# RG-LRU gates in a decoder layer: both gates of a block as the columns of one matmul, high and low half of its input in one stack of 128 rows

## The chip, the core and the metric

One NeuronCore of one Trainium2 chip runs the whole kernel. The metric is the device time of one execution in microseconds. The kernel before was timed in three runs: median 2068.51 us, from 2068.23 to 2069.02. A profile of one more execution goes with them; every row of a trace below is from it.

## The reference

One layer of a decoder: 512 tokens of 2048 features, float32. One input projection makes `rg_x`, `rg_gate`, `q`, `k` and `v`. The changed part is the recurrent group, 1024 features wide, whose two gates are matrices of 16 blocks of 64x64:

```python
def _rglru_group(rg_x, rg_gate, conv_w, conv_b, wa, ba, wx, bx, lam):
    u = _causal_dwconv(rg_x, conv_w, conv_b)
    ub = u.reshape(B, S, RG_BLOCKS, RG_BLOCK_DIM)          # 16 blocks of 64
    r = sigmoid(einsum('bsgi,gij->bsgj', ub, wa).reshape(B, S, RG_WIDTH) + ba)
    ig = sigmoid(einsum('bsgi,gij->bsgj', ub, wx).reshape(B, S, RG_WIDTH) + bx)
    log_a = RG_C * r * log_sigmoid(lam)
    a = exp(log_a)
    mult = sqrt(-expm1(2.0 * log_a))
    h = scan(h = a * h + mult * ig * u)                    # along the tokens
    return h * gelu(rg_gate)
```

Beside it a differential attention of 8 heads with two softmaxes each; then an output projection over both groups, a layer norm, a gated MLP of width 5632 with a causal convolution of width 3, and a second layer norm.

## The kernel before

Activations lie transposed: a tile is 128 features by 512 tokens. Float32 accuracy is had from a cheaper matmul type by splitting each operand into a high half (a copy in the rounded type) and a low half (the difference): `split`, ScalarE for the copy (L108), VectorE for the difference (L109). A product is then three matmuls, high by high, high by low, low by high (`mm3`, L115). Weights come by DMA as 128x1024 raw tiles, are split by the same two lines into `whi` and `wlo`, and are used four matmul triples per 512 columns.

A list `PLAN` sets the order of the first stage: projections of `v`, `q` and `k` of a head, `rg_x` ("x"), `rg_gate` ("g") and, four times, "rec": the recurrence over two tiles of 128 features. Attention and recurrence are generators that are started some microseconds of modelled time later, so that their instructions fall among the matmuls of the next projections. A scheduler then orders each engine's instructions by modelled times; each engine takes them in that order.

- `rg_in` (the "x" step) makes `u` of one tile: ScalarE from PSUM (L448), three convolution steps on VectorE (L452), then a split into a 128x512 `hi` and `lo`.
- `recurrence` takes two tiles, four gates. For each gate of each tile there is a 128x128 matrix with two 64x64 blocks on its diagonal and zeros elsewhere, split into high and low: three matmuls and one sigmoid of 128x512 from PSUM (L468).
- After the four sigmoids: exp (L474) and tanh (L476) on ScalarE, `ig * u` on GpSimd (L480), two steps on VectorE (L482, L483), a square root on ScalarE (L486), a product (L488) and the scan (L490, tile `hh`) on VectorE.
- Sigmoid, exp with tanh, and square root need different function tables; ScalarE loads a table (1.28 us) at each change.

The blocks of the four gate matrices of one recurrence are one DMA of 128x512, `gate_w`, split once.

```python
for i, (uu, s) in enumerate(us):
    for g in range(2):
        c = slice((2 * i + g) * P, (2 * i + g + 1) * P)
        pg = bank()
        mm3(pg, (hi[:, c], lo[:, c]), s, True, True)
        gt = t_tile(F32, "gt")
        nc.scalar.activation(gt, pg, AF.Sigmoid, bias=col((C_BA, C_BX)[g] + j0 + i))
        gates.append(gt)
```

Of the kernel before, what the change touches and what calls it, by code (L numbers as in the profile page):

```python
# [10 lines left out]
F32 = mybir.dt.float32  # L11
F32R = mybir.dt.float32r
AF = mybir.ActivationFunctionType
ALU = mybir.AluOpType
PSUM = bass.MemoryType.PSUM

P = 128
# [4 lines left out]
RGT = RG // P  # L22
H = 8
DH = 64
# [12 lines left out]
C_BA = C_CONVB + RGT  # L37
C_BX = C_BA + RGT
# [5 lines left out]
C_FB = C_FW + 2 * FT * 3  # L44
C_LQ = C_FB + 2 * FT
NC_ = C_LQ + 4 * DH


A_BUFS = 56
# [22 lines left out]
def f32(ap):  # L72
    return ap.bitcast(F32)
# [3 lines left out]
def trunk_kernel(ctx, tc, xT, w_qkg, w_v, gate_w, w_out0, w_out, w_up0, w_up, w_down, ln2, consts, out):  # L77
    nc = tc.nc
# [10 lines left out]
    def bank():  # L89
        return psum.tile([P, S], F32, tag="ps", bufs=8, name="ps")  # L90

    def a_tile(dt=F32R, name="a"):
        return act.tile([P, S], dt, tag="a", bufs=A_BUFS, name=name)

    def t_tile(dt=F32, name="t"):
        return tmp.tile([P, S], dt, tag="t", bufs=T_BUFS, name=name)
# [7 lines left out]
    def split(src, hi=None, lo=None, mk=a_tile):  # L104

        hi = mk(F32R, "hi") if hi is None else hi
        lo = mk(F32R, "lo") if lo is None else lo
        nc.scalar.activation(hi, src, AF.Copy)  # L108
        nc.vector.tensor_tensor(lo, src, f32(hi), ALU.subtract)  # L109
        return hi, lo  # L110

    def mm3(ps, w, x, first, last, onto=False):

        for n, (a, b) in enumerate(((w[0], x[0]), (w[0], x[1]), (w[1], x[0]))):
            nc.tensor.matmul(  # L115
                ps, a, b, start=first and n == 0, stop=last and n == 2, skip_group_check=onto
            )
# [82 lines left out]

    cst = const.tile([P, NC_], F32, name="cst")

    def col(i, n=1):
        return cst[:, i : i + n]
# [126 lines left out]
    def proj():  # L331

        ps = bank()
        for half in range(2):
            parts = W.take()
            for kk in range(8):
                kt = half * 8 + kk
                hi, lo = parts[kk // 4]
                c = slice((kk % 4) * P, (kk % 4 + 1) * P)
                mm3(ps, (hi[:, c], lo[:, c]), x[kt], kt == 0, kt == KT - 1)  # L340
                if kt < KT - 1:
                    tick(TK)
        return ps
# [101 lines left out]
    def rg_in(j):  # L445
        ps = proj()
        uu = t_tile(F32, "uu")
        nc.scalar.activation(  # L448
            uu, ps, AF.Identity, scale=col(C_CONVW + 4 * j + 3), bias=col(C_CONVB + j)
        )  # L450
        for t in range(1, 4):
            nc.vector.scalar_tensor_tensor(  # L452
                uu[:, t:], ps[:, : S - t], col(C_CONVW + 4 * j + 3 - t), uu[:, t:],
                ALU.mult, ALU.add,
            )
        return uu, split(uu, mk=t_tile)

    def recurrence(j0, us, w):

        hi, lo = w  # L460
        gates = []
        for i, (uu, s) in enumerate(us):
            for g in range(2):
                c = slice((2 * i + g) * P, (2 * i + g + 1) * P)
                pg = bank()
                mm3(pg, (hi[:, c], lo[:, c]), s, True, True)
                gt = t_tile(F32, "gt")
                nc.scalar.activation(gt, pg, AF.Sigmoid, bias=col((C_BA, C_BX)[g] + j0 + i))  # L468
                gates.append(gt)
        ms, as_ = [], []  # L470
        for i in range(2):
            j, r = j0 + i, gates[2 * i]
            a = t_tile(F32, "a")
            nc.scalar.activation(a, r, AF.Exp, scale=c8[:, j : j + 1])  # L474

            nc.scalar.activation(r, r, AF.Tanh, scale=nc8[:, j : j + 1])  # L476
            as_.append(a)
        for i in range(2):
            uu, ig, r, a = us[i][0], gates[2 * i + 1], gates[2 * i], as_[i]
            nc.gpsimd.tensor_tensor(ig, ig, uu, ALU.mult)  # L480
            m = t_tile(F32, "m")
            nc.vector.tensor_tensor(m, a, a, ALU.mult)  # L482
            nc.vector.scalar_tensor_tensor(m, m, 1.0, r, ALU.add, ALU.mult)  # L483
            ms.append(m)
        for m in ms:
            nc.scalar.activation(m, m, AF.Sqrt)  # L486
        for i in range(2):
            nc.vector.tensor_tensor(ms[i], ms[i], gates[2 * i + 1], ALU.mult)  # L488
            hh = a_tile(F32, "hh")
            nc.vector.tensor_tensor_scan(hh, as_[i], ms[i], 0.0, ALU.mult, ALU.add)  # L490
            mix[j0 + i] = hh
        yield 0.0
# [57 lines left out]
    us = {}  # L550
# [87 lines left out]
    for dt in range(KT):  # L638
# [14 lines left out]
        if dt == 1:  # L653
            pair = [bank(), bank()]
            for u in range(KT // 4):
                parts = W.take()
                for kk in range(4):
                    i = 4 * u + kk
                    tick(2 * TK)
                    assert ms[i] is not None  # L660
                    hi, lo = parts[kk // 2]
                    for o in range(2):
                        c = slice((kk % 2 * 2 + o) * P, (kk % 2 * 2 + o + 1) * P)
# [11 lines left out]
        for n in range(2):  # L675
            parts = W.take()
            for kk in range(8):
                i = n * 8 + kk
                hi, lo = parts[kk // 4]
                c = slice((kk % 4) * P, (kk % 4 + 1) * P)  # L680
                mm3(ps, (hi[:, c], lo[:, c]), ms[i], i == 0, i == KT - 1)
        residual(dt, ps)
    for tok in halves:
        for dt in range(KT - 2, KT):
            ps = bank()
            for i in range(KT):
                hi, lo = wl[dt - KT + 2][i // 8][i % 8 // 4]
                c = slice((i % 4) * P, (i % 4 + 1) * P)
# [230 lines left out]
    for i in range(2, PLAIN):  # L919
        pss = []  # L920
        for g in range(2):
            ps = bank()
            for half in range(2):
# [4 lines left out]
                for kk in range(8):  # L928
                    kt = half * 8 + kk
                    hi, lo = parts[kk // 4]  # L930
                    c = slice((kk % 4) * P, (kk % 4 + 1) * P)
# [47 lines left out]
    at = 0  # L979
# [70 lines left out]
def _layout(inputs):  # L1050
    import numpy as np

    g = {k: np.asarray(v) for k, v in inputs.items()}
    f = np.float32

    def tiles(w, cols):

        k = w.shape[0] // P
        w = w.reshape(k, P, -1, P)
        return np.ascontiguousarray(w.transpose(2, 1, 0, 3)[cols]).reshape(len(cols), P, k * P)  # L1060

    a = {}
    a["xT"] = np.ascontiguousarray(g["x"][0].T).reshape(KT, P, S)
    w = g["w_in"][0]
    rgx, rgg = list(range(0, 8)), list(range(8, 16))
    qk = [t for h in range(H) for t in (16 + h, 24 + h)]
    a["w_qkg"] = tiles(w, qk + rgx + rgg)
    wv = w[:, 4096:].reshape(KT // 2, 2, P, 2, 512)
    a["w_v"] = np.ascontiguousarray(wv.transpose(3, 0, 2, 1, 4)).reshape(2, KT // 2, P, 1024)
    gw = np.zeros((RGT // 2, P, 2, 2, P), f)  # L1070
    for i, n in enumerate(("rg_gate_a_w", "rg_gate_x_w")):
        b = g[n][0].reshape(RGT // 2, 2, 2, 64, 64)
        gw[:, :64, :, i, :64] = b[:, :, 0].transpose(0, 2, 1, 3)
        gw[:, 64:, :, i, 64:] = b[:, :, 1].transpose(0, 2, 1, 3)
    a["gate_w"] = gw.reshape(RGT // 2, P, 4 * P)
    wo = g["w_out"][0].reshape(KT, P, D)[ORDER].reshape(D, D)
    a["w_out"] = tiles(wo, list(range(2, KT)))
    w = wo.reshape(KT // 4, 4, P, KT, P)[:, :, :, :2]
    a["w_out0"] = np.ascontiguousarray(w.transpose(0, 2, 1, 3, 4)).reshape(KT // 4, P, 1024)
    up = [t for i in range(FT) for t in (i, FT + i)]  # L1080
    a["w_up"] = tiles(g["w_up"][0], up[4:])
    w = g["w_up"][0].reshape(2, KT // 2, P, 2 * FT, P)[:, :, :, up[:4]]
    a["w_up0"] = np.ascontiguousarray(w.transpose(1, 2, 0, 3, 4)).reshape(KT // 2, P, 1024)
    wd = g["w_down"][0].reshape(FT // 2, 2, P, D // S, S)
    parts, at = [], 0
    for n in CHUNKS:
        w = wd[at // 2 : (at + n) // 2].transpose(3, 0, 2, 1, 4)
        parts.append(w.reshape(-1, P, 2 * S))
        at += n
    a["w_down"] = np.ascontiguousarray(np.concatenate(parts))  # L1090
    a["ln2"] = np.stack([g["ln_ffn_g"][0], g["ln_ffn_b"][0]]).astype(f)
    c = np.zeros((P, NC_), f)

    def put(at, v):
        c[:, at : at + v.shape[1]] = v

    put(C_CONVW, g["rg_conv_w"][0].reshape(4, RGT, P).transpose(2, 1, 0).reshape(P, -1))
    for at, n in ((C_CONVB, "rg_conv_b"), (C_BA, "rg_gate_a_b"), (C_BX, "rg_gate_x_b"),
                  (C_LAM, "rg_lambda"), (C_SUB, "subln_g"), (C_G1, "ln_mix_g"),
                  (C_B1, "ln_mix_b")):  # L1100
        put(at, g[n][0].reshape(-1, P).T)
    fw = g["ffn_conv_w"][0].reshape(3, 2 * FT, P)[:, up]
    put(C_FW, fw.transpose(2, 1, 0).reshape(P, -1))
    put(C_FB, g["ffn_conv_b"][0].reshape(2 * FT, P)[up].T)
    for i, n in enumerate(("lam_q1", "lam_k1", "lam_q2", "lam_k2")):
        put(C_LQ + i * DH, np.broadcast_to(g[n][0], (P, DH)))
    a["consts"] = c
    return a
# [23 lines left out]
```

## Time and profile before

| what | value |
|---|---|
| median of three runs | 2068.51 us |
| the profiled execution's own time | 2069.49 us |
| its span, first to last instruction | 2067.7 us |
| TensorE busy | 2048.1 us, 10649 matmuls |
| VectorE busy | 1368.9 us |
| ScalarE busy | 1039.5 us |
| GpSimd busy | 181.4 us |
| mean granted TensorE clock | 0.997 of full speed |

Busy times are read from the page; engines overlap, and matmuls overlap each other, so TensorE's 99% says that it rarely runs dry and not that every matmul is worth its length. The time of a dense stream is read from starts, one to the next. In a timeline an instruction that waited carries in brackets how long its engine was idle before it and whose result ended the wait. The chain of waits goes back from the end, at each step to what released it. ScalarE, VectorE and GpSimd are called ACT, DVE and POOL in the rows, TensorE PE, and its weight load PEld. "L115" is a line of the kernel before; in the changed kernel the lines of helpers stand one further down.

### The profile page before, as it was taken

The numbers are of one execution on the slowest core, as the hardware profiler recorded it, in microseconds if no ns is written. First come the engines' busy times: TensorE is split into PE (matmuls) and PEld (weight loads), VectorE is DVE, ScalarE is ACT, GpSimd is POOL, SyncE is SP. The second block draws the span as 40 slices with busy tenths as digits, with TensorE's granted clock in tenths as the row PEclk, the third lists the DMA queues.
The fourth block names the chain that finished last, engine by engine and source line by source line (L and its number), as shares of the span: only waits on it lengthen the run. The fifth ranks groups of instructions, "written<-read, shape, count | busy, mean of one in ns | idle before, by whom it ended". The sixth has DMA issues, their size and how long they took to land.

```text
span 2067.7 us, 28020 instructions
## 1 busy us (share of the span) xinstructions
PE 2048.1 (99%) x10649; PEld 1757.5 (85%) x10649; DVE 1368.9 (66%) x2075; ACT 1039.5 (50%) x1651; POOL 181.4 (9%) x227
## 2 busy tenths in 40 slices
PE   9999999999999999999999999999999999999997
PEld 7888888888888899888888888888888888888886
DVE  6566645768334867888888888888888343333346
ACT  5475735668322656566565566566566232222232
POOL 1000000010122232001001000000100000000000
PEclk9999999999999999999999999999999999999999
DMA  6223222222443246576676676676678643242322
GB/s 221 97 72 97 73 93 85 87 82 91 144 128 128 76 125 167 153 189 171 167 192 170 166 188 176 165 187 178 164 184 283 225 139 116 92 142 92 112 82 82
DMA packets 98152, 288.46 MB, mean 140 GB/s; under 512 B 10209, under 2 KB 18401, under 8 KB 98017
## 3 DMA queue, kind: packets, MB, share of 16 engines
q1 hardware_dynamic: 86496, 244.71, 36.2%
q0 software_dynamic: 11520, 41.95, 11.9%
q8 instruction: 84, 1.38, 0.3%
q14 instruction: 52, 0.42, 0.1%
HBM read 266.70 MB, written 19.92 MB: 139 GB/s over the span
## 4 chain that ended last, share of the span: by engine, by line
PE 94%; ACT 3%; DVE 2%; DMA 1%; issue 1%; DVEq 0%; SPq 0%; ACTq 0%
PE ps L115 54%; PE ps L129 37%; PE ps L359 1%; ACT gt L468 0%; PE ps L360 0%; PE ps L765 0%; ACT s L371 0%; PE ps L389 0%; DVE lo L109 0%; DVE y L621 0%; DMA hid<-hidd 0%; ACT a L474 0%; ACT L486 0%; ACT L474 0%; ACT L468 0%
## 5 line engine op out<-in xcount | busy, mean ns | idle before, releaser
L109 DVE TENSOR_TENSOR wlo<-raw,whi 128x512 fp32r<-128x512 f32 (+1 forms) x676 | 605.2, 913 | 408.6 <-ACT whi L108 407.1
L108 ACT ACTIVATE whi<-raw 128x512 fp32r<-128x512 f32 (+1 forms) x676 | 525.3, 801 | 477.4 <-PE ps L115 376.6
L129 PE MATMUL ps<-hl,whi 128*128 128x512 f32 x1280 | 320.5, 392 | 0.0
L115 PE MATMUL ps<-wlo,hi 128*128 128x512 f32 x768 | 299.5, 390 | 0.6 <-DVE wlo L109 0.6
L115 PE MATMUL ps<-whi,hi 128*128 128x512 f32 x768 | 299.1, 390 | 0.3 <-ACT hi L108 0.3
L115 PE MATMUL ps<-hi,whi 128*128 128x512 f32 (+1 forms) x768 | 298.9, 389 | 0.0
L115 PE MATMUL ps<-whi,lo 128*128 128x512 f32 x768 | 298.7, 389 | 0.0
L115 PE MATMUL ps<-hi,wlo 128*128 128x512 f32 (+1 forms) x768 | 296.6, 386 | 1.2 <-DVE wlo L109 1.2
L115 PE MATMUL ps<-lo,whi 128*128 128x512 f32 (+1 forms) x768 | 296.2, 386 | 0.0
L129 PEld LDWEIGHTS ps<-hl,whi 128*128 128x128 f32 x1280 | 230.2, 189 | 41.1
L129 PE MATMUL ps<-x,whi 128*128 128x512 f32 x960 | 237.2, 389 | 0.0
L129 PEld LDWEIGHTS ps<-x,whi 128*128 128x128 f32 x960 | 180.1, 188 | 37.3
L129 PE MATMUL ps<-hl,wlo 128*128 128x256 f32 x1280 | 173.0, 283 | 0.0
L115 PEld LDWEIGHTS ps<-hi,wlo 128*128 128x128 f32 x768 | 144.3, 188 | 31.3 <-DVE wlo L109 2.4
L115 PEld LDWEIGHTS ps<-whi,hi 128*128 128x128 f32 x768 | 144.3, 188 | 30.9 <-ACT hi L108 1.0
L115 PEld LDWEIGHTS ps<-wlo,hi 128*128 128x128 f32 x768 | 144.4, 188 | 30.8 <-DVE wlo L109 1.0
L115 PEld LDWEIGHTS ps<-whi,lo 128*128 128x128 f32 x768 | 144.4, 188 | 30.0
L115 PEld LDWEIGHTS ps<-lo,whi 128*128 128x128 f32 x768 | 144.5, 188 | 27.5 <-issue 0.2
L129 PEld LDWEIGHTS ps<-hl,wlo 128*128 128x128 f32 x1280 | 164.6, 192 | 3.5 <-ACT cu L878 0.4
L115 PEld LDWEIGHTS ps<-hi,whi 128*128 128x128 f32 x768 | 144.4, 188 | 27.2 <-ACT whi L108 0.2
L129 PEld LDWEIGHTS ps<-x,wlo 128*128 128x128 f32 x960 | 131.0, 190 | 9.4
L807 POOL DMA_DIRECT2D raw<-in_w_up x80 | 69.6, 874 | 735.9 <-DVE raw L827 402.3
(206 smaller groups left out, 2363.8 us busy)
## 6 DMA issues: line engine op xcount, KB each, us to landing
raw<-in_w_up SPq DMA_DIRECT2D x176, 512.0 KB, 5.1
raw<-in_w_down SPq DMA_DIRECT2D x88, 512.0 KB, 3.6
raw<-in_w_up POOLq DMA_DIRECT2D x80, 512.0 KB, 6.8
raw<-in_w_qkg SPq DMA_DIRECT2D x64, 512.0 KB, 3.6
raw<-in_w_out SPq DMA_DIRECT2D x32, 512.0 KB, 3.7
hidd<-cv SPq DMA_DIRECT2D x44, 256.0 KB, 3.9
hid<-hidd SPq DMA_DIRECT2D x44, 256.0 KB, 5.3
raw<-in_w_v SPq DMA_DIRECT2D x15, 512.0 KB, 4.5
```

The source lines that it names most:

```text
L108: nc.scalar.activation(hi, src, AF.Copy)
L109: nc.vector.tensor_tensor(lo, src, f32(hi), ALU.subtract)
L115: nc.tensor.matmul(ps, a, b, start=first and n == 0, stop=last and n == 2, skip_group_check=onto)
L129: nc.tensor.matmul(o, a, b, start=not onto and k == 0, stop=k == len(steps) - 1, skip_group_check=onto)
L359: nc.tensor.matmul(ps[:, :L], qs, k[c][:, :L], start=True, stop=False)
L807: nc.gpsimd.dma_start(self.raw[name], w_up[2 * (self.i - 2) + g][:, n * 1024 : (n + 1) * 1024], accum_op=ALU.add,)
```

## The change

A block of 64 features is now multiplied in two matmuls for both gates. Its 64 rows of `u` are stacked twice in a tile of 128 rows: high half in the block's own rows, low half in the other 64. The weight has the same 64x128 block twice, one above the other; its columns are the 64 of one gate and the 64 of the other. High weights times the stack give high by high plus high by low in one matmul. For low by high the low weights are zeroed in the rows that face the low half, and one more matmul is added. The result holds both gates of a block, one above the other; each is written by its own 64-row sigmoid into the rows where the old gate tile has it, so that the rest of the recurrence stays as it is. For the second block of a tile the order of the gates' columns is turned round.

```diff
@@ rg_in
-        return uu, split(uu, mk=t_tile)
+        stacks = [t_tile(F32R, "st") for _ in range(2)]
+        for st, own, other in zip(stacks, SIDES, SIDES[::-1]):
+            nc.scalar.activation(st[own], uu[own], AF.Copy)
+            nc.vector.tensor_tensor(st[other], uu[own], f32(st[own]), ALU.subtract)
+        return uu, stacks
@@ recurrence
         hi, lo = w
+        for own, block in zip(SIDES[::-1], range(2)):
+            z = f32(lo).rearrange("p (i b c) -> p i b c", i=2, b=2)
+            nc.gpsimd.memset(z[own, :, block, :], 0.0)
         gates = []
-        for i, (uu, s) in enumerate(us):
-            for g in range(2):
-                c = slice((2 * i + g) * P, (2 * i + g + 1) * P)
+        for i, (uu, stacks) in enumerate(us):
+            gts = [t_tile(F32, "gt") for _ in range(2)]
+            for b, st in enumerate(stacks):
+                c = slice((2 * i + b) * P, (2 * i + b + 1) * P)
                 pg = bank()
-                mm3(pg, (hi[:, c], lo[:, c]), s, True, True)
-                gt = t_tile(F32, "gt")
-                nc.scalar.activation(gt, pg, AF.Sigmoid, bias=col((C_BA, C_BX)[g] + j0 + i))
-                gates.append(gt)
+                nc.tensor.matmul(pg, hi[:, c], st, start=True, stop=False)
+                nc.tensor.matmul(pg, lo[:, c], st, start=False, stop=True)
+                own = SIDES[b]
+                for gt, rows, at in zip(gts, (own, SIDES[1 - b]), (C_BA, C_BX)):
+                    nc.scalar.activation(gt[own], pg[rows], AF.Sigmoid, bias=col(at + j0 + i)[own])
+            gates.extend(gts)
@@ _layout: gate_w, same size (128 x 512 per recurrence), other arrangement
+    gw = np.stack([g[n][0] for n in ("rg_gate_a_w", "rg_gate_x_w")], 2).reshape(RGT // 2, 4, DH, 2, DH)
+    gw[:, 1::2] = gw[:, 1::2, :, ::-1].copy()
+    gw = gw.reshape(RGT // 2, 4, DH, P).transpose(0, 2, 1, 3).reshape(RGT // 2, DH, 4 * P)
+    a["gate_w"] = np.ascontiguousarray(np.concatenate([gw, gw], 1)).astype(f)
```

`SIDES` are the slices of rows 0 to 63 and 64 to 127. What the change makes of the order is the same at all four recurrences; the first is shown. ScalarE before, from the split of the second tile's `u` (`hi<-uu`) to the next weight copies (`gt` are gates, `s` scores of attention, `a` and `m` the coefficients of the recurrence, `wt` attention weights):

```order
L108 ACTIVATE hi<-uu 128x512
L468 ACT_TABLE_LOAD
L468 ACTIVATE gt<-ps,cst 128x512
L371 ACT_TABLE_LOAD
L371 ACTIVATE s,den<-s,nmx 128x512 x2
L468 ACT_TABLE_LOAD
L468 ACTIVATE gt<-ps,cst 128x512 x3
L474 ACT_TABLE_LOAD
L474 ACTIVATE a<-gt,c_87 128x512 x2
```

ScalarE now, the same stretch:

```order
L460 ACTIVATE st<-uu 64x512 x2
L482 ACT_TABLE_LOAD
L482 ACTIVATE gt<-ps,cst 64x512
L372 ACT_TABLE_LOAD
L372 ACTIVATE s,den<-s,nmx 128x512 x2
L482 ACT_TABLE_LOAD
L482 ACTIVATE gt<-ps,cst 64x512 x7
L488 ACT_TABLE_LOAD
L488 ACTIVATE a<-gt,c_87 128x512 x2
```

The table loads stand where they stood; three sigmoids between two of them have become seven, and one copy two. VectorE now, from the squared `a` to the weight split behind the scan (`hh` is the scan's result, `wlo` the low half of weights):

```order
L496 TENSOR_TENSOR m<-a 128x512 x2
L497 SCALAR_TENSOR_TENSOR m<-m,gt 128x512 x2
L397 TENSOR_TENSOR wt<-ps,wt 128x4x128
L502 TENSOR_TENSOR m<-m,gt 128x512 x2
L504 SCALAR_TENSOR_TENSOR hh<-a,m 128x512 x2
L110 TENSOR_TENSOR wlo<-raw,whi 128x512
L523 SCALAR_TENSOR_TENSOR q<-ps,q 64x512
```

Nothing moved here: before, VectorE has the same seven rows in the same order. Earlier in its row, the two 64-row subtracts of a tile stand between the two score maxima of the attention, where one 128-row subtract stood ahead of both; and at the first tile the two transposes of attention weights that follow from those maxima stand three matmuls later on TensorE. TensorE before, at the end of the attention values (`wt`), with the matmul by `ones_r` that sums squares over a head:

```order
L115 MATMUL ps<-wt,hi 128x256 x2
L115 MATMUL ps<-wt,vl 128x256
L115 MATMUL ps<-hi,whi 128x512
L115 MATMUL ps<-lo,whi 128x512
L115 MATMUL ps<-hi,wlo 128x512
L115 MATMUL ps<-hi,whi 128x512
L115 MATMUL ps<-lo,whi 128x512
L115 MATMUL ps<-hi,wlo 128x512
L115 MATMUL ps<-hi,whi 128x512
L115 MATMUL ps<-lo,whi 128x512
L437 MATMUL ps<-hi,ones_r 128x512
L115 MATMUL ps<-hi,wlo 128x512
```

TensorE now, the same place:

```order
L116 MATMUL ps<-wt,hi 128x256 x2
L116 MATMUL ps<-wt,vl 128x256
L116 MATMUL ps<-hi,whi 128x512
L116 MATMUL ps<-lo,whi 128x512
L438 MATMUL ps<-hi,ones_r 128x512
L116 MATMUL ps<-hi,wlo 128x512
```

Six projection matmuls that stood behind the attention values now stand ahead of them; the `hi,wlo` behind `ones_r` is the same matmul in both.

## Rows read from the trace of the kernel before

**Rows 1.** The page, part 1: busy us, share of the span, instructions.
```profile
PE 2048.1 (99%) x10649; PEld 1757.5 (85%) x10649; DVE 1368.9 (66%) x2075; ACT 1039.5 (50%) x1651; POOL 181.4 (9%) x227
```
**Rows 2.** Timeline, TensorE, first recurrence: start us, us, instruction [idle before, releaser].
```profile
101.43 0.39 PE L115 MATMUL ps<-hi 128*128 128x512 f32 x1
101.66 0.39 PE L115 MATMUL ps<-lo,hi 128*128 128x512 f32 x1
...
118.79 0.51 PE L437 MATMUL ps<-hi,ones_r 128*128 128x512 f32 x1
119.57 0.50 PE L115 MATMUL ps<-hi,wlo 128*128 128x512 f32 x1 [0.27 <-DVE wlo L109]
```
**Rows 3.** Chain of waits, first recurrence: start us, us, what.
```profile
102.31 0.69 ACT gt L468
...
107.15 1.84 ACT gt L468 x3
...
117.74 1.20 DVE hh L490
118.94 0.59 DVE wlo L109
...
119.57 2.11 PE ps L115 x8
```
**Rows 4.** Timeline, TensorE, last recurrence.
```profile
425.11 0.50 PE L115 MATMUL ps<-hi,wlo 128*128 128x512 f32 x1 [0.29 <-DVE wlo L109]
```
**Rows 5.** Timeline, VectorE, first recurrence.
```profile
118.85 0.66 DVE L109 TENSOR_TENSOR wlo<-raw,whi 128x512 fp32r<-128x512 f32 x1
```
**Rows 6.** Groups by line and shape, 82 to 130 us: busy us, mean ns | idle before.
```profile
L109 DVE TENSOR_TENSOR lo<-uu,hi 128x512 fp32r<-128x512 f32 x2 | 1.4, 691 | 1.5 <-ACT hi L108 1.5
...
L508 ACT ACTIVATE q<-ps 64x512 fp32r<-64x512 f32 x2 | 1.2, 586 | 0.5 <-DVE q L509 0.5
...
L109 DVE TENSOR_TENSOR k<-ps,k 64x512 fp32r<-64x512 f32 x1 | 0.7, 676 | 0.0
...
L432 ACT ACTIVATE sq<-ps 128x512 f32<-128x512 f32 x1 | 0.6, 598 | 0.3 <-PE ps L115 0.3
```
**Rows 7.** Timeline, ScalarE, first recurrence.
```profile
99.82 0.63 ACT L108 ACTIVATE hi<-uu 128x512 fp32r<-128x512 f32 x1 [1.81 <-DVE uu L452]
100.47 1.28 ACT L468 ACT_TABLE_LOAD   x1
102.31 0.69 ACT L468 ACTIVATE gt<-ps,cst 128x512 f32<-128x512 f32 x1 [0.56 <-PE ps L115]
...
115.72 1.14 ACT L108 ACTIVATE whi<-raw 128x512 fp32r<-128x512 f32 x2
...
118.12 0.62 ACT L108 ACTIVATE hi<-sq 128x512 fp32r<-128x512 f32 x1
```
**Rows 8.** Timeline, VectorE, ahead of the first recurrence.
```profile
87.93 0.69 DVE L109 TENSOR_TENSOR lo<-uu,hi 128x512 fp32r<-128x512 f32 x1 [0.76 <-ACT hi L108]
...
94.28 0.17 DVE L376 RECIPROCAL rec<-den 128x2 f32<-128x2 f32 x1 [1.37 <-ACT s L371]
```
**Rows 9.** Timelines of VectorE (split of the gate weights) and GpSimd.
```profile
75.50 0.69 DVE L109 TENSOR_TENSOR lo<-raw,hi 128x512 fp32r<-128x512 f32 x1
...
96.22 0.36 POOL L420 MEMSET wt<- 128x128 f32 x2 [82.69 <-PE ps L115]
```
**Rows 10.** Timeline, TensorE, behind the first layer norm.
```profile
701.59 0.75 PE L115 MATMUL ps<-x,hi 128*128 128x256 f32 x4 [2.35 <-ACT x L108]
...
704.98 0.58 PE L115 MATMUL ps<-x,hi 128*128 128x256 f32 x1 [2.54 <-DVE x L109]
```
**Rows 11.** Busy us by stretch: stretch us, PE, PEld, DVE, ACT, POOL, granted clock, DMA, GB/s.
```profile
703.00:704.00 1.00, 0.00 (x0) 0.00 (x0) 1.00 (x3) 1.00 (x4) 1.00 (x2) 0.70 0.00 0
...
709.00:710.00 1.00, 1.00 (x6) 1.00 (x6) 1.00 (x4) 0.01 (x1) 0.00 (x0) 0.50 0.85 295
710.00:711.00 1.00, 1.00 (x10) 1.00 (x9) 1.00 (x3) 1.00 (x3) 0.00 (x0) 0.88 0.19 78
```

More of the change, by code (lines that the diff above doesn't have):

```diff
@@ L46 @@
 NC_ = C_LQ + 4 * DH
+SIDES = [slice(0, DH), slice(DH, P)]
 A_BUFS = 56
@@ L1069, in _layout @@
     a["w_v"] = np.ascontiguousarray(wv.transpose(3, 0, 2, 1, 4)).reshape(2, KT // 2, P, 1024)
[L1070 to L1075, printed above, removed]
+    gw = np.stack([g[n][0] for n in ("rg_gate_a_w", "rg_gate_x_w")], 2).reshape(RGT // 2, 4, DH, 2, DH)
+    gw[:, 1::2] = gw[:, 1::2, :, ::-1].copy()
+    gw = gw.reshape(RGT // 2, 4, DH, P).transpose(0, 2, 1, 3).reshape(RGT // 2, DH, 4 * P)
+    a["gate_w"] = np.ascontiguousarray(np.concatenate([gw, gw], 1)).astype(f)
     wo = g["w_out"][0].reshape(KT, P, D)[ORDER].reshape(D, D)
```

## The prediction

> **What bounds the kernel now.** I read the page's busy shares first. TensorE works 99% of the span [rows 1], so whatever moves the end must move TensorE. A dense 128x512 matmul starts 0.227 us after the one before, as the gate matmuls at 101.43 and 101.66 do [rows 2]; its 0.39 us is the pipelined length and must not be summed. Then I read the chain of waits around one call of `recurrence`. The reader is to see that it leaves TensorE at 102.31 and comes back only at 119.57: gate sigmoid, three more sigmoids, further steps of the recurrence on both engines, the scan on VectorE, a weight split `wlo`, and only then a matmul [rows 3]. So for 17 us the chain is ScalarE's and VectorE's. TensorE has other matmuls meanwhile and almost covers it: the `ones_r` matmul starts at 118.79, the next would follow at 119.02, and it starts at 119.57, held by `wlo` [rows 2]. That is a stall of 0.55 us. All four recurrences have it at the same matmul; a row of the last stands for the other three [rows 4].
>
> Why does a weight split wait for a scan? VectorE takes its instructions in order. Its `wlo` at 118.85 follows the scan [rows 5], and the order of the changed program keeps `wlo` behind `hh` in the same way. The split is not late for want of data; it is queued.
>
> **The change part by part.**
>
> *TensorE.* Per recurrence 12 gate matmuls become 8, four recurrences: 16 fewer at 0.227 us, 3.63 us of TensorE time in all, 0.91 us per recurrence. All of them stand ahead of the stalled matmul. Its release does not depend on TensorE's count, so the 0.91 us only makes TensorE arrive earlier and wait longer. I cost this edit at a gain of 0 as long as `wlo` comes last, and at -3.63 us if something else covers the chain.
>
> *Sigmoids.* Per recurrence 4 of 128x512 become 8 of 64x512; after the second sigmoid table load 7 stand where 3 stood. Three took 1.84 us, one alone takes 0.69, so one follows another after (1.84 - 0.69) / 2 = 0.575 us [rows 3]. The trace has no 64-row sigmoid. Bounds from its rows: at the low end half the rows cost half the time (8 x 0.29 = the 2.3 us of before, nothing added); at the high end a half costs as much as a whole. The nearest rows: a 64x512 copy out of PSUM takes 586 ns and a 128x512 square 598 ns [rows 6]. I take the high end: 4 x 0.575 = 2.30 us per recurrence. They stand in the middle of the chain. From the table load at 100.47 to the weight copies at 115.72 ScalarE is idle only once, 0.56 us before the first sigmoid [rows 3, 7], so what is added after that sigmoid has no idle time to vanish in and reaches `wlo` whole.
>
> The Trainium skill, "ScalarE: Activation LUTs", section "What ACT_TABLE_LOAD costs", prices an activation with a bias column at about 280 ns plus 0.833 ns per element of a row, with some 93 ns of overlap, and has no term for how many rows are active. My estimate from it is 614 ns each, 2.45 us per recurrence and 9.8 us in all against 9.2 from the rows; the trace agrees within 7% on the pitch, and on the half tile by its copies alone.
>
> *Split of u.* One 128x512 copy becomes two of 64x512 (one more at about 0.53 us of pitch) and one subtract becomes two; a 64-row subtract takes 676 ns, a 128-row one 691 [rows 6]. For the second tile the extra copy starts right behind the one at 99.82 and pushes the first sigmoid table load by 0.53 us; the 0.56 us of idle before the first sigmoid hides exactly that [rows 7], since that sigmoid waited for TensorE. If the cover is gone it costs 0.5 us per recurrence. For the first tile VectorE gets one more operation of about 0.6 us at 87.93, ahead of the score maxima. The new order has the transposes that hang on them three matmuls (0.68 us) later, and VectorE's next idle piece of 1.37 us takes up most [rows 8]. I carry 0.2 us per recurrence on to the second tile's `u` and with it into the chain, between 0 (the idle takes all) and 0.6 (it takes none).
>
> *Zeroing.* Two GpSimd memsets per recurrence on a tile split at 75.50, wanted by TensorE at 101.43; GpSimd does nothing until its `wt` memset at 96.22 [rows 2, 9]. What hides them is these 20 us. Nothing is queued behind them that is wanted sooner. Cost 0. With nothing to hide them they would cost TensorE one or two memsets of some 0.2 us each.
>
> *Moved matmuls.* The four transposes and the attention values stand some matmuls later than before; with the same work ahead of the stalled matmul this only changes where in the wait TensorE idles.
>
> *Sum.* 2.30 + 0.2 = 2.5 us per recurrence, times 4 = +10.0 us, nothing off for the matmuls. The profiled execution took 2069.49 us (span 2067.7, 1.8 around it): 2079.5. It lay 1.0 us above the median of the three timed runs, so I predict a median of **2078.5 us**. What is late next: inside the longer wait also the second-half weight `whi`, copied at 115.72, and `hi` of `sq` at 118.12 [rows 7], come 2.3 us later, so the idle time will be in three or four pieces, of which `wlo` remains the last. Behind it VectorE, ScalarE and TensorE are all shifted alike, so I see no place where the 10 us are won back.
>
> **The rivals.**
>
> *TensorE's count decides (the other side).* 16 matmuls less and the waits hidden: 2068.51 - 3.63 = 2064.9, and with the four stalls of 0.55 us gone too 2062.7. For it: 99% busy. Against it: the stall that exists already, at the place where ScalarE's work grows. It decides only if `wlo` could be taken ahead of the scan, or if the chain became more than 0.91 us shorter per recurrence; nothing in the new order does either.
>
> *Half a tile costs half.* If a 64-row sigmoid takes 0.29 us, the chain keeps its length, `wlo` keeps its time, the removed matmuls are spent waiting: 2068.5, up to 2070.5 with the VectorE operation. For it: the trace has no such sigmoid. Against it: the 586 against 598 ns.
>
> *The clock falls in the longer wait.* TensorE arrives at 119.02 - 0.91 = 118.1 and is let go at 119.57 + 2.5 = 122.1, so it idles about 4.0 us in pieces. The trace has one such place in the middle of the program: two idle pieces of 2.35 and 2.54 us with a little work between, ending at 704.98 [rows 10], and the granted clock fell from 1.00 to 0.50 (2.4 to 1.2 GHz) during the second and stayed there to about 710.2 [rows 11]. Work from 704.98 to 710.2 at half the clock lost 2.6 us. Four times that is 10.4 us: 2088.9; one or two falls give 2081 to 2084. Against it: the pieces are shorter here and 4.0 is less than 4.9 us; the stalls of 0.55 us so far cost no clock.
>
> The Trainium skill, "TensorE: Matmul & The Clock Gate", section "HAM oscillation — how this bites in real kernels", warns that idle gaps between bursts of matmuls return the engine to its lower clock. By that rule this rival is the forecast's natural companion; the trace agrees at 704, and no run here yet shows it in a recurrence.
>
> **How the numbers follow.** Chain longer by 2.3 to 3.1 us per recurrence, clock steady: 0.60, 2077.7 to 2081. The same with the clock falling in some recurrences: 0.25, 2081 to 2089. Half a tile costs half, or the chain is taken up somewhere: 0.10, near 2068.5. TensorE's count: 0.05, 2062.7 to 2065. What cannot be told from no change is 0.2% or 4.1 us. Slower than that: the first two, 0.85. Within it: the third and most of the fourth, 0.12. Faster: 0.03. The range leaves out the last two cases and the top of the second: 2072 to 2087; the likeliest case alone is 2076 to 2081.
>
> **What would show it.** In the changed profile the last sigmoids should be a group of seven per recurrence with a mean near 0.68 us each on 64x512, taking about 4.1 us where three took 1.84; the exp behind them should come about 2.5 us later after its first sigmoid. TensorE's wait for `wlo` should grow from 0.3 us in the list of waits to several us over four places, with waits for `whi` and for `hi` of `sq` beside it, and TensorE's busy time should fall though the span grows. TensorE should have 16 matmuls less. The two memsets per recurrence should stand near the split of the gate weights, far ahead of the gates. The granted clock at the four places says whether the third rival adds to it. I am wrong if the 64-row sigmoids take about half, if the matmul after `ones_r` is no longer released by `wlo`, or if the span shrinks.

## The result and the profile after

The changed kernel takes 2086.28 us (median of three runs, 2086.23 to 2087.54) against 2068.51: 1.0084 of before, 95% interval 1.007 to 1.0098. It is slower by 17.8 us, where +10.0 was forecast. The profiled execution took 2086.23 us (span 2084.1) against 2069.49 (2067.7), so the two traces have to account for 16.4 us of span. In the rows of the changed kernel the lines of the recurrence stand 14 further down. Medians of the experiments leave out four executions of 2279 us and more, two of the kernel before and two of `before_late_tail_fewer`.

The page's busy shares after, to hold against [rows 1]:

```profile
PE 2050.3 (98%) x10633; PEld 1757.3 (84%) x10633; DVE 1373.8 (66%) x2083; ACT 1056.1 (51%) x1675; POOL 183.8 (9%) x235
```

The 16 matmuls are gone (10649 to 10633), and yet the time is longer. Busy time of TensorE hardly tells anything here: it rose by 2.2 us, in part since some matmuls ran at half the clock (below).

ScalarE's timeline after, first recurrence, to hold against [rows 7]:

```profile
100.00 1.29 ACT L460 ACTIVATE st<-uu 64x512 fp32r<-64x512 f32 x2 [2.21 <-DVE uu L453]
101.30 1.28 ACT L482 ACT_TABLE_LOAD   x1
102.59 0.68 ACT L482 ACTIVATE gt<-ps,cst 64x512 f32<-64x512 f32 x1
...
107.42 4.93 ACT L482 ACTIVATE gt<-ps,cst 64x512 f32<-64x512 f32 x7
...
119.07 1.13 ACT L109 ACTIVATE whi<-raw 128x512 fp32r<-128x512 f32 x2
...
121.07 0.62 ACT L109 ACTIVATE hi<-sq 128x512 fp32r<-128x512 f32 x1
```

Seven half sigmoids take 4.93 us where three whole ones took 1.84: +3.09. The two copies of `u` take 1.29 us where one took 0.63, and the first sigmoid no longer waits for TensorE: the idle 0.56 us is filled. The chain of waits gives the starts of the sigmoids one by one:

```profile
107.42 0.69 ACT gt L482
...
108.13 0.69 ACT gt L482
108.84 0.68 ACT gt L482
...
122.29 0.59 DVE wlo L110
```

One starts 0.71 us after the one before ((4.93 - 0.69) / 6), although each takes the same 0.69 as a whole one. Whole ones followed after 0.575, so they overlapped; these don't. Behind the scan stands the same `wlo` as in [rows 3], 3.35 us after its old time.

TensorE's timeline at the same place ([rows 2] before):

```profile
116.75 0.38 PE L116 MATMUL ps<-wt,hi 128*128 128x256 f32 x1 [0.84 <-ACT wt L396]
117.60 0.39 PE L116 MATMUL ps<-wt,hi 128*128 128x256 f32 x1 [0.46 <-DVE wt L397]
...
119.74 0.50 PE L116 MATMUL ps<-hi,whi 128*128 128x512 f32 x1 [0.56 <-ACT whi L109]
...
121.74 0.50 PE L438 MATMUL ps<-hi,ones_r 128*128 128x512 f32 x1 [1.27 <-ACT hi L109]
122.93 0.80 PE L116 MATMUL ps<-hi,wlo 128*128 128x512 f32 x1 [0.69 <-DVE wlo L110]
```

The one stall of before has become five, each at an operand that ScalarE or VectorE makes behind the sigmoids. The list of TensorE's waits after (us in total, times, longest) shows that all four recurrences have them:

```profile
PE ps L438 <- ACT hi L109: 5.1, 4, 1.3
PE ps L116 <- DVE wlo L110: 3.4, 5, 0.7
PE ps L116 <- ACT wt L396: 3.3, 4, 0.8
...
PE ps L116 <- ACT whi L109: 2.2, 4, 0.6
PE ps L116 <- DVE wt L397: 1.9, 4, 0.5
```

In the same list of before, the only entry from the recurrences is this one (four of its five times; the fifth, 0.6 us, is elsewhere and stays):

```profile
PE ps L115 <- DVE wlo L109: 1.8, 5, 0.6
```

Where the 16.4 us arise is read from the first gate matmul of each recurrence and the span's end:

| us | 1st | 2nd | 3rd | 4th | span |
|---|---|---|---|---|---|
| before | 101.43 | 205.50 | 353.02 | 406.96 | 2067.7 |
| after | 101.21 | 209.90 | 362.28 | 419.79 | 2084.1 |
| later by | -0.22 | 4.40 | 9.26 | 12.83 | 16.4 |
| added since | | 4.62 | 4.86 | 3.57 | 3.57 |

The third and fourth recurrence add 3.57 us each, the first two 1.05 and 1.29 more. The granted clock tells these apart. Stretches of 1 us after, columns as in [rows 11]; the first four lie at the end of the first recurrence's waits and behind it, then two at the second recurrence and one at the third:

```profile
122.00:123.00 1.00, 0.31 (x2) 0.07 (x1) 0.97 (x3) 0.73 (x2) 0.00 (x0) 0.79 0.00 0
123.00:124.00 1.00, 1.00 (x3) 0.81 (x4) 0.97 (x2) 0.38 (x1) 0.00 (x0) 0.50 0.00 0
...
125.00:126.00 1.00, 1.00 (x4) 0.80 (x3) 0.97 (x2) 0.39 (x1) 0.00 (x0) 0.51 0.70 111
126.00:127.00 1.00, 1.00 (x6) 0.78 (x5) 0.97 (x2) 0.23 (x1) 0.00 (x0) 1.00 0.85 303
...
231.00:232.00 1.00, 0.39 (x1) 0.36 (x2) 0.97 (x2) 0.41 (x1) 0.00 (x0) 0.90 0.00 0
...
233.00:234.00 1.00, 1.00 (x4) 0.82 (x3) 0.97 (x2) 1.00 (x2) 0.00 (x0) 0.50 0.00 0
...
384.00:385.00 1.00, 1.00 (x4) 0.85 (x5) 0.97 (x2) 0.32 (x1) 0.00 (x0) 1.00 0.00 0
```

The clock fell from 1.00 to 0.50 (2.4 to 1.2 GHz) during the last wait of the first recurrence, and just behind that of the second, which ended at 231.61; each time it came back some 3.4 us later. In the other two recurrences it stayed at 1.00. Before, it fell in none.

### The profile page after: what moved, and what is told of

The parts are those of the page before. It is cut to its first block, busy times and chain, and to the rows that moved or that the text cites. A ratio compares the mean times of both kernels' runs of the same rounds, so it can differ in the third digit from the quotient of the medians.

```text
span 2084.1 us, 28049 instructions
## 1 busy us (share of the span) xinstructions
PE 2050.3 (98%) x10633; PEld 1757.3 (84%) x10633; DVE 1373.8 (66%) x2083; ACT 1056.1 (51%) x1675; POOL 183.8 (9%) x235
## 3 DMA queue, kind: packets, MB, share of 16 engines
q8 instruction: 84, 1.38, 0.3%
## 4 chain that ended last, share of the span: by engine, by line
PE 91%; ACT 4%; DVE 4%; DMA 1%; issue 1%; DVEq 0%; POOL 0%; ACTq 0%; SPq 0%
PE ps L116 52%; PE ps L130 37%; ACT gt L482 1%; ACT s L372 1%; ACT L482 0%; DVE wlo L110 0%; DVE uu L453 0%; PE ps L360 0%; PE ps L779 0%; DVE s L363 0%; PE ps L361 0%; DMA raw<-in_w_down 0%; DVE y L635 0%; DMA hid<-hidd 0%; ACT a L488 0%
```

## The experiments

All ratios are against the kernel before, timed beside each experiment.

**One suspect at a time.** Is it the half sigmoids alone? `half_sigmoids` is the kernel before with only this (`col(...)` stands for the same bias column in both):

```diff
-                nc.scalar.activation(gt, pg, AF.Sigmoid, bias=col(...))
+                for rows in SIDES:
+                    nc.scalar.activation(gt[rows], pg[rows], AF.Sigmoid, bias=col(...)[rows])
```

> The kernel before with one edit: each gate's sigmoid is done as two of 64x512, low rows then high rows; twelve gate matmuls, the old split and the old weights stay. Theory (the chain through the sigmoids sets the time): seven half sigmoids take 4.9 us where three whole ones took 1.84, so the weight split wlo and the matmul behind ones_r come 3.1 us later in each recurrence: 2068.5 + 4 x 3.1 = 2080.9, with a fall of the clock in one or two waits 2082 to 2084. Rival (the stacked operands, the memsets or the moved matmuls make the changed kernel slow): 2068.5.

Measured: 2087.74 us against 2069.62, 1.0088 (1.0073 to 1.0103). The seven sigmoids and the stalled matmul in its timelines (ScalarE, TensorE):

```profile
106.67 4.90 ACT L470 ACTIVATE gt<-ps,cst 64x512 f32<-64x512 f32 x7
```

```profile
122.30 0.80 PE L116 MATMUL ps<-hi,wlo 128*128 128x512 f32 x1 [0.42 <-DVE wlo L110]
```

From the first sigmoid (101.84) to that matmul it is 20.46 us, against 17.26 before and 20.34 after. With all its matmuls and its old split this kernel is as slow as the changed one, so the sigmoids suffice. Its time exceeds what was expected because the clock fell in three of the four recurrences. Its first gate matmuls start at 100.96, 210.75, 361.43 and 419.99, and its span is 2085.6; read as in the table above, the recurrences add 5.72, 3.16, 4.62 and 4.90 us. The 3.16 belongs to the one without a fall and is the 3.1 of the theory. The 5.72 belongs to the first, where the clock stayed at 0.50 from 121 to 128 us, twice as long as in the others:

```profile
121.00:122.00 1.00, 0.78 (x1) 0.27 (x1) 1.00 (x2) 1.00 (x3) 0.00 (x0) 0.58 0.00 0
...
127.00:128.00 1.00, 1.00 (x3) 0.73 (x3) 0.68 (x1) 0.29 (x1) 0.00 (x0) 0.51 0.47 106
```

`half_sigmoids_grouped` has the same eight instructions, the four lower halves first and then the four upper ones (the lines that only make the list `late` are left out):

```diff
-                nc.scalar.activation(gt, pg, AF.Sigmoid, bias=col(...))
+                late.append((gt, pg, col(...)))
+        for rows in SIDES:
+            for gt, pg, bias in late:
+                nc.scalar.activation(gt[rows], pg[rows], AF.Sigmoid, bias=bias[rows])
```

> As the run with half sigmoids, but the four low halves first and then the four high halves, so that most follow one with the same rows. If any operation on 64 rows starts only when the one before it has ended (0.70 us each), the same as that run: 7 in 4.9 us, 2081 to 2084. If only a change of the rows costs the overlap: 5 of the 6 successions at 0.575 us and one at 0.70, 7 in 4.3 us, chain 2.4 us longer, 2068.5 + 9.7 = 2078.2.

```profile
106.86 4.25 ACT L473 ACTIVATE gt<-ps,cst 64x512 f32<-64x512 f32 x7
```

Seven in 4.25 us in place of 4.90: with one change of rows left, five of the six pitches are 0.575 and one 0.71, which gives 0.69 + 2.88 + 0.71 = 4.28. Same instruction, same shape, other order: a 64-row sigmoid overlaps the one before it if both use the same half of the rows, and not if they change between the lower and the upper half. The total came to 2087.01 us (2083.59 to 2087.58; 1.008, 1.0065 to 1.0095), above both expectations. The profiled execution is the fastest of the four, and even there the clock fell in three recurrences. The mean clock goes from 0.995 (2083.59) down to 0.991 in the slower ones, so more falls of the clock are the likely reason why the median shows little of the gain; their traces were not taken. The chain's gain stands in the trace: 19.81 us from first sigmoid to stalled matmul.

`whole_sigmoids` is the opposite cut: the changed kernel with one sigmoid of 128x512 per bank. It leaves out the sorting of rows into their gates.

```diff
-                for gt, rows, at in zip(gts, (own, SIDES[1 - b]), (C_BA, C_BX)):
-                    nc.scalar.activation(gt[own], pg[rows], AF.Sigmoid, bias=col(at + j0 + i)[own])
+                nc.scalar.activation(gts[b], pg, AF.Sigmoid, bias=col((C_BA, C_BX)[b] + j0 + i))
```

> The changed kernel, but one sigmoid of 128x512 for each gate bank, four per recurrence instead of eight; this leaves out the sorting of rows into the two gates. Stacks, memsets and eight matmuls stay. Theory (sigmoids on the chain): three whole sigmoids take 1.84 us again, only the second copy of u and the later u are left, about 0.5 us per recurrence: 2070.5, none of the 3.6 us of the removed matmuls seen. Rival (TensorE's count decides): 2064.9. Rival (stacks or memsets are what costs): 2080 or more.

Measured: 2073.09 us, 1.0017 (1.0007 to 1.0026).

```profile
108.83 1.85 ACT L480 ACTIVATE gt<-ps,cst 128x512 f32<-128x512 f32 x3
```

From first sigmoid to stalled matmul it is 17.28 us, the length of before. So some 14 of the changed kernel's 17.8 us are the sigmoids. The fewer matmuls give nothing back here: TensorE waits for `hi` of `sq` 4.9 us over the four recurrences. The clock fell in the first two. In the profiled execution these add 1.8 and 1.9 us from first gate matmul to first gate matmul, the other two 0.5 and 0.4. So the theory's 0.5 us holds where the clock stayed, and the falls make most of the 2.6 us by which the median exceeds the expected 2070.5.

`halved_split` is the kernel before with `u` split in two halves of 64 rows, as the change does it:

```diff
-        return uu, split(uu, mk=t_tile)
+        hi, lo = t_tile(F32R, "hi"), t_tile(F32R, "lo")
+        for own in SIDES:
+            nc.scalar.activation(hi[own], uu[own], AF.Copy)
+            nc.vector.tensor_tensor(lo[own], uu[own], f32(hi[own]), ALU.subtract)
+        return uu, (hi, lo)
```

> The kernel before with the split of u done in two halves of 64 rows, two copies and two subtracts instead of one each. Theory: the two copies do not overlap (0.65 us each), VectorE is 0.2 us late at the second tile, so the first sigmoid and with it wlo come 0.5 us later per recurrence: 2070.5. Rival (the 0.56 us of idle before the first sigmoid hides it): 2068.5.

Measured: 2071.91 us, 1.0013 (1.0004 to 1.0023), +2.3 us between the medians.

```profile
102.51 1.28 ACT L459 ACTIVATE hi<-uu 64x512 fp32r<-64x512 f32 x2 [2.23 <-DVE uu L453]
103.81 1.28 ACT L473 ACT_TABLE_LOAD   x1
105.11 0.69 ACT L473 ACTIVATE gt<-ps,cst 128x512 f32<-128x512 f32 x1
```

The copies, too, don't overlap (1.28 for two of 0.63) and close the idle time before the first sigmoid. The split is a second, smaller cost of some 0.6 us per recurrence.

**Does TensorE's count matter?** `before_fewer_matmuls` leaves out the low-by-high matmul of the gates, 16 fewer as in the change.

```diff
-                mm3(pg, (hi[:, c], lo[:, c]), s, True, True)
+                nc.tensor.matmul(pg, hi[:, c], s[0], start=True, stop=False)
+                nc.tensor.matmul(pg, hi[:, c], s[1], start=False, stop=True)
```

> The kernel before with 16 gate matmuls fewer and nothing else: each gate leaves out its third matmul (low weights by high input), two instead of three per gate. Theory (the matmul behind ones_r is let go by ScalarE's and VectorE's chain): no gain, 2068.5, TensorE waits up to 0.9 us longer per recurrence; the first bank is ready 0.23 us earlier, so at most 4 x 0.23 = 0.9 us are gained. Rival (TensorE's count decides): 2068.5 - 3.6 = 2064.9.

Measured: 2068.41 us against 2069.3, 0.9996 (0.9987 to 1.0005): no gain that can be told from none, certainly not 3.6 us. The waits show where they went:

```profile
PE ps L437 <- ACT hi L108: 2.1, 4, 0.5
PE ps L115 <- DVE wlo L109: 1.8, 5, 0.6
```

The `wlo` entry is what it was before; a new one for `hi` of `sq` takes up the freed time.

`before_late_tail` puts `yield 6.0` ahead of the exp, so that the steps behind the sigmoids are ordered 6 us of modelled time later, behind other work. `before_late_tail_fewer` has that and the missing matmuls.

```diff
                 gates.append(gt)
+        yield 6.0
         ms, as_ = [], []
```

> The kernel before, with a pause of 6 modelled us in recurrence between the sigmoids and exp: the weight copies and splits of the next projections then stand ahead of exp, square root and scan on ScalarE and VectorE. Theory: the stall of 0.55 us goes in all four recurrences, 2068.5 - 2.2 = 2066.3. If the wait only moves to a later weight split: 2068 to 2070.

> The kernel before with both edits: the pause of 6 modelled us, and 16 gate matmuls left out (low weights by high input). Theory: once the wait is gone TensorE's count decides, 3.6 us under the run with the pause alone: 2062.7. If some wait is left at the recurrences: no difference between the two.

The first took 2071.18 us, 1.0008 (0.9999 to 1.0017): a miss. The four stalls at `wlo` were gone, but others had come:

```profile
PE ps L359 <- ACT k L520: 2.1, 4, 0.9
PE ps L437 <- DVE lo L109: 1.7, 2, 0.9
...
PE ps L115 <- DVE wlo L109: 0.6, 1, 0.6
```

What was taken out of one wait came back in another here. The second took 2067.05 us, 0.9991 (0.9982 to 1.0). That is 4.1 us under the first by the medians and 3.5 by the ratios, where 3.6 were expected: with the stall at `wlo` gone, TensorE's count shows, as it did not in the order of before. The time itself, 2062.7 expected, was missed with that of the first.

**A way out.** The same pause in the changed kernel, at 6, 10 and 14; then 14 with the sigmoids sorted by rows as well, and the kernel before with 14.

> The changed kernel with the same pause of 6 modelled us between the sigmoids and exp. Theory: TensorE no longer waits behind the longer sigmoids, no fall of the clock, and the 16 removed matmuls count: 2062.7, faster than both kernels and 23 us under the changed kernel. Rival (eight half sigmoids ahead of the weight copies still hold them back by some us): 2068 to 2076.

> The changed kernel with a pause of 10 modelled us between the sigmoids and exp. With 6 the waits behind wlo went, but in the third and fourth recurrence the low half of the squares (lo of sq) was queued behind the product and the scan, two waits of 2 us with a fall of the clock in one. Here it stands ahead of the scan in all four. Theory (what is queued behind the tail decides): the 4 us and the clock's 1.7 go, 2074.7 - 5 = 2069.5. Rival (the wait moves again): 2074.

> The same with a pause of 14: the reciprocal of rs too stands ahead of the recurrence's tail. Theory: no wait of TensorE of over 0.5 us is left at the recurrences, 2064 to 2067, so that the 16 removed matmuls show at last. Rival: the tail now stands before the copies of k, and TensorE waits there, 2070 to 2074.

> The same with a pause of 14, and the eight sigmoids in an order in which each second one has the same rows, in and out, as the one before. If the same rows let two overlap (0.575 us apart instead of 0.70): the last seven take 4.5 us instead of 4.9, and TensorE gains at most 0.4 us per recurrence: the same as without to 1.6 us less.

> The kernel before with a pause of 14. Theory: its stall of 0.55 us per recurrence goes, 2066.3, and the changed kernel with the same pause lies up to 3.6 us under it. If the eight half sigmoids still hold something back, the changed kernel lies level or above.

| kernel | median us | ratio to before | 95% |
|---|---|---|---|
| changed, pause 6 (`after_late_tail`) | 2074.74 | 1.0025 | 1.0016 to 1.0034 |
| changed, pause 10 | 2066.69 | 0.999 | 0.9981 to 0.9999 |
| changed, pause 14 | 2067.98 | 0.9996 | 0.9987 to 1.0005 |
| changed, pause 14, sorted | 2067.6 | 0.9996 | 0.9987 to 1.0005 |
| before, pause 14 | 2070.69 | 1.0009 | 1.0001 to 1.0018 |

Pause 6 came out in its rival's range. It left one bad wait in two recurrences: `lo` of `sq` now stands behind the scan on VectorE, and in the last recurrence the clock fell after it (433 to 438 us), though not after the longer one in the third.

```profile
376.69 0.50 PE L438 MATMUL ps<-lo,ones_r 128*128 128x512 f32 x1 [2.21 <-DVE lo L110]
...
432.84 0.51 PE L438 MATMUL ps<-lo,ones_r 128*128 128x512 f32 x1 [1.91 <-DVE lo L110]
```

With pause 10, VectorE's timeline in the first recurrence has the weight splits and the split of `sq` ahead of the steps behind the exp, and so ahead of the scan:

```profile
118.36 1.29 DVE L110 TENSOR_TENSOR wlo<-raw,whi 128x512 fp32r<-128x512 f32 x2
119.58 0.68 DVE L110 TENSOR_TENSOR lo<-sq,hi 128x512 fp32r<-128x512 f32 x1
...
122.02 1.38 DVE L497 TENSOR_TENSOR m<-a 128x512 f32<-128x512 f32 x2 [1.16 <-ACT a L489]
```

TensorE's list of waits then has two entries from this part of the program (0.6 us of the second is the one elsewhere), and the clock stays at 1.00 in all four recurrences:

```profile
PE ps L360 <- ACT k L534: 2.4, 5, 0.7
...
PE ps L116 <- DVE wlo L110: 0.9, 3, 0.6
```

The seven sigmoids still take 4.87 us there, and nobody waits for them. This is the fastest kernel of the study by its median, 2.8 us better than expected and 2.0 us under before; that is less than can be called a gain at the 0.2% of the prediction, though its interval ends just below 1. Pause 14 came out 1 us above its expected range. Sorting the sigmoids shortens them as worked out (three pitches of 0.575, three of 0.71 and the last 0.69 give 4.5):

```profile
107.45 4.50 ACT L486 ACTIVATE gt<-ps,cst 64x512 f32<-64x512 f32 x7
```

Each of these seven reads another PSUM bank than the one before it, whether the rows change or not, so it is not the bank that decides. The gain is worth nothing measurable once the chain is off TensorE's way. The kernel before with 14 was a miss, 2070.69 where 2066.3 was expected: its waits for `wlo` at the recurrences went, and TensorE waits for the copies of `k` instead, 3.3 us in all. At the same pause of 14 the changed kernel lies 2.7 us under it: that is most of its 3.63 us of matmuls. Before with a pause of 10 was not run, so what the change is worth at the best order of each is open.

## Why the prediction was right, and where its sum fell short

The direction, the mechanism and the range held, but not the likeliest case of the prediction, a steady clock and 2076 to 2081. The measured 2086.28 lies 0.7 us inside the upper end of the range, which reached so far because a fall of the clock was allowed for; without one, the 3.57 us per recurrence would already have given about 2083. By its own steps, per recurrence where nothing else is said:

- **TensorE's count, 0 as long as `wlo` comes last.** Right. `before_fewer_matmuls` gained nothing; only with the tail moved did 16 matmuls show (3.5 to 4.1 us).
- **Sigmoids, 4 x 0.575 = 2.30 us.** This term was mis-sized: it measured 3.09, 3.2 us too little in all. That a half costs as much as a whole was right (0.69 against 0.69). What failed is taking the pitch of whole ones for the halves. The pitch of 0.575 holds an overlap that goes when the rows change, and in the changed order either the rows read or the rows written change at each sigmoid. So six intervals are 0.13 us longer each, which is the 0.79 that the term lacked. The Trainium skill, "ScalarE: Activation LUTs", section "What ACT_TABLE_LOAD costs", gives successive activations an overlap of about 93 ns without a condition. The traces agree for equal rows (0.69 less 0.575 is some 0.11) and disagree where rows change (0.71, no overlap), so the estimate from it, 2.45 us, fell short in the same way. The trace of before could have told this. Its own 64-row activations are copies of the halves of `q` and `k`. The copy of the lower half of `q` at 117.64 ends 0.10 us after the next activation has started at 118.12 [rows 7]; that of the upper half at 120.27 has ended before the next one starts:

```profile
117.64 0.58 ACT L508 ACTIVATE q<-ps 64x512 fp32r<-64x512 f32 x1
...
120.27 0.59 ACT L508 ACTIVATE q<-ps 64x512 fp32r<-64x512 f32 x1 [0.49 <-DVE q L509]
120.88 1.15 ACT L108 ACTIVATE whi<-raw 128x512 fp32r<-128x512 f32 x2
```

So the overlap is not lost by going from 64 rows to 128 as such; it is lost here behind an upper half.

- **Split of u, 0.2 us.** Measured 0.5: from the first gate matmul to the first sigmoid it is 1.38 us after (101.21 to 102.59) and 0.88 before. 0.10 is the second copy, which at 0.66 us was longer than the idle 0.56 that was to hide it. The rest is `u` of the second tile: its copy starts at 100.00 against 99.82 [rows 7], though the first tile's `u` began 0.19 us earlier than before (83.28 against 83.47), so it is 0.37 late. VectorE's second subtract is behind that. Its rows after show the pair, 0.70 us longer than the one subtract of [rows 8], and the reciprocal with its idle time unchanged at 1.37, so that idle took nothing up:

```profile
87.75 1.39 DVE L461 TENSOR_TENSOR st<-uu,st 64x512 fp32r<-64x512 f32 x2 [0.42 <-ACT st L460]
...
94.72 0.17 DVE L377 RECIPROCAL rec<-den 128x2 f32<-128x2 f32 x1 [1.37 <-ACT s L372]
```

- **Zeroing, 0.** Right; GpSimd's row has both memsets done 20 us ahead of its next work, and the gates never wait for them:

```profile
76.07 0.66 POOL L471 MEMSET lo<- 64x256 f32 x2 [62.42 <-DVE lo L110]
```

- **The clock falls in the longer wait.** Given as a rival with 0.25, it joined the forecast in two recurrences of four, at 1.05 and 1.29 us each where up to 2.6 was allowed, 2.3 in all. The Trainium skill, "TensorE: Matmul & The Clock Gate", section "HAM oscillation — how this bites in real kernels", warns that idle gaps between bursts of matmuls put the engine back to its lower clock; its example has one long wait per tile. The trace agrees in two recurrences, with five short waits each, and shows the same waits without a fall in the other two.

The sum with measured terms: 4 x (3.09 + 0.50) + 2.3 = 16.7 us, less 0.2 by which the first gate matmul came earlier, against 16.4 of span. The five waits for `wt`, `whi`, `hi` and `wlo` are how the delay shows on TensorE, not a cost beside it. The prediction named three of these operands; the two `wt` of the attention were not foreseen. One sign was wrong: TensorE's busy time was to fall, and it rose by 2.2 us.

What stays open: why the clock fell in two recurrences and not in the others, whose waits are alike to 0.1 us in the trace; and why in `half_sigmoids` it fell in three, and in the first of them stayed low for twice as long.

## What to carry to other kernels

Price a cut in one engine's work by who releases that engine at this place: 16 matmuls fewer were worth nothing until the chain of ScalarE and VectorE behind them was ordered out of the way, and then they were worth about what the count says. Splitting these activations by rows doubled their cost (a half starts 0.575 us after the one before, like a whole one), and where the halves alternated it was more than double (0.71 us); if it must be, keep equal rows together or put the chain where nobody waits for it. Before a cut is given up, try where the longer chain stands: here one pause in the order took the changed kernel from 2086.3 to 2066.7 us, five times what the 16 matmuls could bring.

## What the runs showed of the hardware that was not expected

Successive 64-row activations of ScalarE overlap by about 0.11 us when they use the same half of the rows, and not when the rows read or the rows written change between the lower and the upper half (pitch 0.575 against 0.71; seven halves in 4.25, 4.50 or 4.90 to 4.93 us by order alone). Copies do the same: a lower and an upper half take 1.28 to 1.29 us, two whole ones 1.13. A 128-row activation after a lower half does overlap it (117.64 and 118.12 in the kernel before), one after an upper half does not (120.27 and 120.88). Whether it is the first row that counts was not tested.

The clock can fall in or just behind waits shorter than those of the layer norm: after one of 1.91 us at 432.84 with pause 6, and in `whole_sigmoids` in two recurrences whose waits are 1.2 and 0.3 to 0.4 us. It mostly stayed at 0.50 for some 3.4 us then, and that cost 1.05 to 1.29 us in the changed kernel; once, in `half_sigmoids`, it stayed for 6.8 us, and that cost 2.6 (5.72 less 3.16).

The start of the program is not steady: the first step of `u` began at 83.47 us before, at 83.28 after, and at 85.45 in `halved_split`. Times of two traces are therefore compared here from one place inside the stretch, never from the span's start.
